# Expert outputs stored in two channel halves, their two planes summed by matrix products, and the loop for further tokens placed ahead of the last expert's down products

## The chip, the cores and the metric

The kernel runs on one core of one Trainium2 chip. The metric is device time in microseconds (us) of one launch. The core has five engines that run their own instruction streams in order and wait on semaphores: PE (TensorE, matrix products), DVE (VectorE), ACT (ScalarE), POOL (GpSimd) and SP (SyncE, which only issues transfers here). Sixteen DMA engines move data between memory and SBUF.

## The reference, cut to what matters

Two blocks of a network run on 512 tokens of 1,024 channels. The first ends in a mixture of 32 experts: each token goes to two of them, and the two results, each weighted, are added to the residual stream.

```python
def hierarchical_moe(h, ...):
    ...                                   # two experts and two gates for each token
    def run_block(args):                  # one expert on the tokens that chose it
        tok, e = args
        xb = hf[jnp.minimum(tok, n_tok - 1)]
        a = xb @ w_gate[e]
        b = xb @ w_up[e]
        return (jax.nn.silu(a) * b) @ w_down[e]
    out = lax.map(run_block, (slot_tok..., block_expert))
    out = out * slot_gate[:, None]
    y = zeros.at[slot_tok].add(out)       # each token: the sum of its two experts' rows

x = x + gate_f * hierarchical_moe(h, ...)
return rms_norm(x, final_g)               # end of the first block
# the second block begins:
x = x + gmlp_mixer(rms_norm_2(x, a_norm), a_w_in, ...)   # uv = gelu(h @ w_in): 1024 -> 2048
```

## The kernel before

**Layout.** Activations are kept with channels on the partitions (`xT`, eight tiles of 128 channels x 512 tokens). Most matrix products run as three (`mm3`): each operand is split into a rounded part and its remainder by ACT (the rounded part, `act`, line 416) and DVE (the remainder, `stt` or `tt`, lines 427 and 419). All code is written in the order in which each engine runs it (`manual_schedule`); nothing reorders it later.

**The experts** (`experts`) run as 19 units; a unit is one expert with up to 128 tokens or a pair with 64 each. Weights stream in through a ring of 15 places (`Ring`, lines 340 and 346, issued by SP). For a unit, the token rows are gathered from memory (line 1493, POOL), turned, multiplied by the gate and up weights, gated, turned again (`act_t`), and multiplied by the down weights (`down`) in two channel halves of 512 (`g` = 0, 1). DVE copies each half from PSUM into `yo` while multiplying by `gate_f`, and when both halves are there POOL scatters the rows with one indirect transfer (`scatter`, line 1498) into `y2` in memory: 2 x 512 rows of 1,024 channels, a plane for a token's first expert and a plane for its second. Ahead of the last unit's `act_t` and `down`, `self.ws.fill()` lets SP request the next stage's first two weight tiles (line 240, 1,024 KB each).

**The loop for further tokens** (`overflow`, line 1612) follows. It serves experts that got more tokens than a unit holds. Its count is read from memory by every engine (line 1611); in the profiled run it is zero, so that no instruction of its body runs. The loop's frame makes every engine wait, on entry and exit, for the semaphores of all transfers issued before it and for all engines.

**Combining** (`combine`) reads the two planes back for each of four tiles of 128 tokens, in twelve transfers on SP and ACT (line 1675); POOL adds the planes (line 1686, once DVE), PE turns each 128 x 128 piece (line 1689), DVE adds it to `xT`, and ACT and DVE make the split operand `ht`.

**The next stage** (`gmlp`) multiplies the 512 tokens by `a_w_in`. For `g` = 0 and 1 the group of products is 2 x 16 units: `ci` = 0, 1 (channels 0 to 511, then 512 to 1023), four channel tiles `i`, four token tiles `o`, three products each, 96 in a group. In the first group with `ci` = 0 the order is by token tile, and `ahead(o)` puts the combining of the following token tile in front of the products:

```python
if ci == 0 and ahead and i == 0:
    ahead(o)
```

Two norms need sums of squares over all channels (`stats_add`: a square by ACT, an addition by DVE, for each channel tile and each of two norms, 16 in all). They are queued in `self.late` when the last token tile has been combined, and taken one at each unit by `factors`, which after 21 units has PE sum them over the partitions (16 products of one column) and DVE compute `rcol`, the factor that the results of both groups need.

Of the kernel before, what the change touches and what calls it, by code (L numbers as in the profile page):

```python
# [10 lines left out]
F32 = mybir.dt.float32  # L11
# [3 lines left out]
OP = mybir.AluOpType  # L15
AX = mybir.AxisListType

S = 512
D = 1024
NT = 4  # L20
# [348 lines left out]
class Kern:  # L369
# [204 lines left out]
    def group(self, specs, acts, banks, weights_stationary=True, start=True, stop=True, done=None, ahead=None):  # L574
# [921 lines left out]

    def scatter(self, y, idx):
        self.nc.gpsimd.indirect_dma_start(out=self.y2[:, :], out_offset=bass.IndirectOffsetOnAxis(ap=idx, axis=0),
                                          in_=y, in_offset=None, bounds_check=2 * S - 1, oob_is_err=False)

# [11 lines left out]
    def experts(self):  # L1512

        nc = self.nc
        self.y2 = self.dr.tile([2 * S, D], F32, name="y2")
        self.ring.fill()
# [85 lines left out]
        self.ws.fill()  # L1602
        act_t(NU - 1)
        down(NU - 1)
        self.ws.hold = len(self.ws.order)
        self.ws.run()

    def overflow(self):
# [3 lines left out]
        with tc.For_i(0, n, 1) as i:  # L1612
# [47 lines left out]
            self.gated(yo, yb, ga)  # L1660
            self.scatter(yo, si[:, 0:1])

    def combine(self):

        nc = self.nc
        ya = [[self.slot(2 * t + k, [128, D]) for k in range(2)] for t in range(NT)]
        for t in range(NT):  # L1670
            n = 2 if t < 2 else 1
            for a in range(n):
                c = slice(a * D // n, (a + 1) * D // n)
                for k in range(2):
                    (nc.sync if k else nc.scalar).dma_start(ya[t][k][:, c], self.y2[k * S + t * 128:k * S + (t + 1) * 128, c])
# [4 lines left out]
        def tile(t):  # L1680
            c = slice(t * 128, (t + 1) * 128)
            b = Pair(*[self.bank(i) for i in ((6, 7), (0, 1))[t % 2]])
            xs = [self.xT[:, 4 * a:4 * a + 4, c] for a in range(2)]
            for a in range(2):
                y, y2 = (ya[t][k][:, a * 512:a * 512 + 512] for k in range(2))
                (nc.vector if (t, a) == (3, 1) else nc.gpsimd).tensor_tensor(out=y, in0=y, in1=y2, op=OP.add)  # L1686
            for a in range(2):
                for i in range(4):
                    nc.tensor.transpose(b[:, a, i * 128:i * 128 + 128], ya[t][0][:, a * 512 + i * 128:a * 512 + i * 128 + 128],  # L1689
                                        self.const("ident"))  # L1690
                self.tt(xs[a], b[:, a].rearrange("p (b t) -> p b t", b=4), xs[a], OP.add)
            for i in range(4):
                self.act(ht[i][:, :, 0, c], xs[i // 2][:, 2 * (i % 2):2 * (i % 2) + 2])
            for i in range(4):
                self.tt(ht[i][:, :, 1, c], xs[i // 2][:, 2 * (i % 2):2 * (i % 2) + 2], ht[i][:, :, 0, c], OP.subtract)

        return hl, tile
# [4 lines left out]
    def gmlp(self, hl, tile):  # L1702
# [6 lines left out]
        rcol = self.sb("rcol", [128, NT])  # L1709
        f = {}  # L1710
# [18 lines left out]

        def ahead(t):  # L1730

            if t == 0:
                tile(0)
            if t < NT - 1:
                tile(t + 1)
            if t == NT - 2:
                for dt in range(DT):
# [11 lines left out]
        for g in range(2):  # L1749
            bk = self.banks4(g)  # L1750

# [4 lines left out]

            self.group(self.HALVES, hl, bk, weights_stationary=False, done=done, ahead=None if g else ahead)
        self.drain()
# [351 lines left out]
def build(nc, ap, where):  # L2110
    with tile.TileContext(nc) as tc, ExitStack() as ctx:
# [4 lines left out]
        K.experts()  # L2116
        K.overflow()
        hl = K.gmlp(*K.combine())
# [22 lines left out]
```

## Time and profile before

| | |
|---|---|
| runs of the kernel | 1903.95, 1904.25, 1905.43 us; median 1904.25 us |
| the profiled execution | 1902.73 us, its span 1901.0 us |
| PE busy in the span | 1803.2 us, 95% |
| last down products of the experts begin / end | 740.95 / 744.60 us |
| first product of the next stage | 761.06 us |
| last of its first 192 products done, third group begins | 812.61 us |

Times within the execution count from the start of the span. The profile names an instruction by engine, source line, operation and its tiles (output <- inputs). "Idle before" is the time for which the engine had nothing to run, and the name behind it is what ended that. A queue's own instructions (waits, branches, requests for transfers) carry a q: SPq, PEldq.

### The profile page before, as it was taken

How to read it: one execution, taken by the hardware profiler on the slowest of the kernel's cores; microseconds unless marked ns; L12 is line 12 of the kernel's file. 1: busy time of each engine (PE TensorE's matmuls, PEld its weight loads, DVE VectorE, ACT ScalarE, POOL GpSimd, SP SyncE). 2: the span in 40 equal slices, each digit the busy share in tenths (PEclk: the TensorE clock that was granted, in tenths of full speed). 3: DMA queues.
4: the chain of work that ended last, by engine and by line, in shares of the span. 5: the costliest groups of instructions: out<-in, count | busy, mean ns of one | idle time of the engine just before them, and what ended most of it. 6: DMA issues, size and time to landing. Idle time of an engine off the chain costs nothing.

```text
span 1901.0 us, 21164 instructions
## 1 busy us (share of the span) xinstructions
PE 1803.2 (95%) x8110; PEld 1265.7 (67%) x8110; DVE 850.3 (45%) x1603; ACT 574.9 (30%) x1021; POOL 105.4 (6%) x101
## 2 busy tenths in 40 slices
PE   5988989999989995999999999999999999999997
PEld 4866654444333332788888888887778888888885
DVE  7668841111111111776545234355665654424434
ACT  4555320000000001633333123246666443222221
POOL 3430001000000001000000000000000000000000
PEclk9999889999999998999999999999999999999998
DMA  7534799999999997313222322322111222322221
GB/s 239 223 133 150 273 391 421 420 420 421 421 413 419 402 410 312 121 67 113 108 90 89 111 89 89 100 78 89 55 58 67 89 89 91 109 89 93 107 78 56
DMA packets 66280, 360.77 MB, mean 190 GB/s; under 512 B 10210, under 2 KB 10242, under 8 KB 33410
## 3 DMA queue, kind: packets, MB, share of 16 engines
q1 hardware_dynamic: 59184, 347.81, 47.6%
q0 software_dynamic: 5552, 8.44, 1.3%
q10 hardware_dynamic: 1442, 3.15, 0.4%
q8 instruction: 64, 1.05, 0.2%
q14 instruction: 38, 0.31, 0.0%
HBM read 356.42 MB, written 14.16 MB: 195 GB/s over the span
## 4 chain that ended last, share of the span: by engine, by line
PE 59%; DVE 1%; DMA 0%; ACT 0%; issue 0%; POOL 0%; ACTq 0%; DVEq 0%; POOLq 0%
PE q L407 58%; PE q L2018 0%; PE q L478 0%; DVE t L419 0%; DMA a<-y 0%; DVE a L427 0%; DVE xT L419 0%; DMA y<-a,sidx 0%; DVE w L427 0%; PE q L1689 0%; DVE ht L427 0%; DVE a L419 0%; ACT t L416 0%; POOL a L1686 0%; DVE sqacc L419 0%
## 5 line engine op out<-in xcount | busy, mean ns | idle before, releaser
L407 PE MATMUL q<-t,w 128*128 128x512 f32 (+1 forms) x3192 | 765.5, 397 | 5.8 <-ACT t L416 2.3
L407 PEld LDWEIGHTS q<-t,w 128*128 128x128 f32 (+1 forms) x3192 | 595.2, 189 | 147.1 <-issue 14.7
L419 DVE TENSOR_TENSOR w<-r,w 128x1024 fp32r<-128x1024 f32 (+1 forms) x173 | 208.7, 1226 | 306.8 <-ACT w L416 306.6
L407 PE MATMUL q<-a,w 128*128 128x512 f32 x1440 | 339.1, 395 | 0.0
L407 PEld LDWEIGHTS q<-a,w 128*128 128x128 f32 x1440 | 269.7, 188 | 63.6 <-issue 1.0
L416 ACT ACTIVATE w<-r 128x1024 fp32r<-128x1024 f32 (+1 forms) x173 | 177.2, 1049 | 348.0 <-issue 177.7
L407 PE MATMUL q<-r,a 128*64 128x512 f32 (+4 forms) x352 | 152.4, 569 | 4.2 <-DMA r<-in_we 4.2
L427 DVE SCALAR_TENSOR_TENSOR a<-a,gates,q 128x512 f32<-128x512 f32 x19 | 14.2, 747 | 277.3 <-PE q L407 264.0
L407 PE MATMUL q<-w,t 128*128 128x256 f32 (+1 forms) x672 | 122.1, 337 | 0.0
L416 ACT ACTIVATE gs<-q 128x512 f32<-128x512 f32 (+2 forms) x25 | 13.6, 544 | 351.4 <-PE q L1559 348.1
L407 PE MATMUL q<-t,a 128*64 128x512 f32 (+1 forms) x296 | 112.1, 596 | 7.0 <-DMA t<-in_we 5.3
L407 PEld LDWEIGHTS q<-w,t 128*128 128x128 f32 x672 | 102.9, 191 | 17.9 <-issue 4.1
L407 PE MATMUL q<-w,a 128*64 128x512 f32 x272 | 98.0, 596 | 11.4 <-DMA w<-in_we 11.4
L407 PE MATMUL q<-a,a 128*64 128x512 f32 (+7 forms) x424 | 98.3, 467 | 0.0
L407 PEld LDWEIGHTS q<-r,a 128*64 128x64 f32 (+1 forms) x352 | 52.7, 158 | 53.7 <-issue 44.0
L407 PEld LDWEIGHTS q<-t,a 128*64 128x64 f32 (+1 forms) x296 | 37.0, 152 | 64.9 <-issue 54.7
L419 DVE TENSOR_TENSOR a<-q,sqt 128x512 f32<-128x512 f32 x38 | 26.3, 691 | 115.1 <-PE q L407 110.2
L416 ACT ACTIVATE a<-ht 128x512 fp32r<-128x512 f32 (+1 forms) x60 | 37.8, 633 | 99.6 <-DVE ht L419 74.8
L419 DVE TENSOR_TENSOR xT<-q,xT 128x512 f32<-128x512 f32 x64 | 43.7, 686 | 53.4 <-PE q L407 43.5
L407 PEld LDWEIGHTS q<-a,a 128*128 128x128 f32 (+2 forms) x424 | 46.3, 173 | 30.6 <-issue 24.6
L407 PEld LDWEIGHTS q<-w,a 128*64 128x64 f32 x272 | 29.0, 137 | 55.1 <-issue 34.7
L427 DVE SCALAR_TENSOR_TENSOR w<-r,cols,w 128x256 fp32r<-128x256 f32 x96 | 44.4, 480 | 39.3 <-ACT w L416 39.1
(335 smaller groups left out, 1580.4 us busy)
## 6 DMA issues: line engine op xcount, KB each, us to landing
r<-in_w SPq DMA_DIRECT2D x100, 1024.0 KB, 4.9
t<-in_we SPq DMA_DIRECT2D x52, 1024.0 KB, 13.6
r<-in_we SPq DMA_DIRECT2D x52, 1024.0 KB, 17.9
w<-in_we SPq DMA_DIRECT2D x52, 1024.0 KB, 16.6
a<-in_we SPq DMA_DIRECT2D x72, 512.0 KB, 14.7
r<-in_w_ada SPq DMA_DIRECT2D x48, 512.0 KB, 5.0
r<-in_wa SPq DMA_DIRECT2D x8, 466.0 KB, 5.7
r<-in_w SPq DMA_DIRECT2D x5, 512.0 KB, 3.6
```

The costliest lines, as they stand in the source:

```text
L407: self.nc.tensor.matmul(out, lhsT=l, rhs=r, start=start, stop=stop)
L416: return self.nc.scalar.activation(out, in_, f, **kw)
L419: return self.nc.vector.tensor_tensor(out=out, in0=a, in1=b, op=op)
L427: return self.nc.vector.scalar_tensor_tensor(out, a, s, b, op0=op0, op1=op1, **kw)
```

## The change

1. `y2` becomes two arrays of 512 channels, `y2[0]` and `y2[1]`. `scatter` takes the half `g` and is called within the loop over `g`: two indirect transfers of half the row where there was one of the whole.
2. `overflow()` is called between `act_t(NU - 1)` and `down(NU - 1)`; the splitting of the next stage's first weights (`ws.hold`, `ws.run`) moves from the end of `experts` into `combine`, behind the requests for the first half.
3. `combine` reads a half-tile (128 tokens, both planes, 512 channels) in one transfer, eight in all: for half 0 on SP and ACT in turn, for half 1 on SP.
4. POOL's additions go. PE turns each piece by a product with the identity, and the second plane's product adds into the same PSUM place: eight products of 128 x 128 for a half-tile (line 407), where there were four transposes.
5. `ahead` now comes in both `ci` of the first group, with half-tiles: the products with channels 0 to 511 need only half 0. `factors` takes two of the statistics at each unit, eight when half 0 is combined and eight when half 1 is, then has PE sum them; the second group's third and fourth token tiles take the PSUM banks 0 and 1 once `r1` is there.

```diff
-            if ci == 0 and ahead:
+            if ahead:
                 units = [(i, o) for o in range(4) for i in range(len(kts))]
...
-                if ci == 0 and ahead and i == 0:
-                    ahead(o)
+                if ahead and i == 0:
+                    ahead(ci, o)
...
-    def scatter(self, y, idx):
+    def scatter(self, y, g, idx):
...
-        self.y2 = self.dr.tile([2 * S, D], F32, name="y2")
+        self.y2 = [self.dr.tile([2 * S, 512], F32, name=f"y2{g}") for g in range(2)]
...
-            self.scatter(yo, self.sidx[:, i:i + 1])
+                self.scatter(yo, g, self.sidx[:, i:i + 1])
...
         act_t(NU - 1)
+        self.overflow()
         down(NU - 1)
-        self.ws.hold = len(self.ws.order)
-        self.ws.run()
...
+        places = ((0, 1, 2, 4), (6, 7, *((5, 3) if NU % 2 else (3, 5))[::-1]))
+        ya = [[None] * NT for _ in range(2)]
+        for a in range(2):
+            src = self.y2[a][:, :].rearrange("(k t p) c -> t p k c", k=2, t=NT)
+            for t in range(NT):
+                ya[a][t] = self.slot(places[a][t], [128, 2, 512])
+                (nc.scalar if a == 0 and t % 2 else nc.sync).dma_start(ya[a][t], src[t])
+            if a == 0:
+                self.ws.hold = len(self.ws.order)
+                self.ws.run()
...
+            b = self.bank((0, 1, 6, 7)[t])
+            x = self.xT[:, 4 * a:4 * a + 4, c]
             for i in range(4):
-                self.act(ht[i][:, :, 0, c], xs[i // 2][:, 2 * (i % 2):2 * (i % 2) + 2])
...
+                for k in range(2):
+                    self.mm(b[:, i * 128:i * 128 + 128], ya[a][t][:, k, i * 128:i * 128 + 128], self.const("ident"), k == 0, k == 1)
+            self.tt(x, b.rearrange("p (b t) -> p b t", b=4), x, OP.add)
...
-            for _ in range(21):
-                yield
-                if self.late:
-                    self.late.pop(0)()
-            b = self.ps(2)
+            while f["stats"] < 2 * DT:
+                yield
+                for _ in range(2):
+                    if self.late:
+                        self.late.pop(0)()
+                        f["stats"] += 1
+            yield
+            b = Pair(self.bank(0), self.bank(1))
...
-        def ahead(t):
...
+        def ahead(a, t):
...
+            n = NT * a + t
+            if n == 0:
+                tile(0, 0)
+            if n < 2 * NT - 1:
+                tile((n + 1) // NT, (n + 1) % NT)
+            if n in (NT - 1, 2 * NT - 2):
+                for dt in range(4 * a, 4 * a + 4):
                     self.late.append(lambda d=dt: self.stats_add(xT[:, d], d))
...
+            if n == NT - 1:
                 self.bg.append(factors())
...
-        K.overflow()
```

**Place one: PE's stream around the loop.** `q_790`, `q_791` (changed: `q_812`, `q_813`) are the last unit's two down halves, `gs` its activations, `r_` and `t_` the down weights, `a_817` (`a_815`) the first rows read back. Before:

```order
L1559 MATMUL q_788_4202<-cst_70,a_782_4171 128x128 [waits DVE_49]
...
L407 MATMUL q_790_4209<-r_767_4090,gs_4207 64x512 [waits DMAHW4_49,DVE_49,Activation_49]
...
L407 MATMUL q_791_4210<-t_776_4122,gs_4207 64x512 [waits DMAHW6_49,DVE_49]
...
L1611 TENSOR_LOAD overi_3757 [waits DVE_49]
L1612 COMPARE_AND_BRANCH
...
L1612 REGISTER_ALU
...
L1689 MATMUL q_843_4411<-cst_70,a_817_4370 128x128 [waits Pool_49]
```

After the change; the row that ends the loop is where every engine leaves it (`DMAHW` are the semaphores of SP's and ACT's transfers, `DMASW` those of POOL's):

```order
L1560 MATMUL q_788_4257<-cst_70,a_782_4223 128x128 [waits DVE_49]
...
L1611 TENSOR_LOAD overi_3797 [waits DVE_49]
L1612 COMPARE_AND_BRANCH
...
L1612 REGISTER_ALU
L1612 COMPARE_AND_BRANCH
L1612 UNCONDITIONAL_BRANCH [waits DMASW5_49,DMASW4_49,DMASW6_49,DMASW3_49,DMASW7_49,DMASW2_49,DMAHW0_49,DMASW1_49,DMAHW1_49,DMASW0_49,DMAHW2_49,SP_sequencer_49,DMAHW3_49,DVE_sequencer_49,DMAHW4_49,PE_sequencer_49,DMAHW5_49,Activation_s
L407 MATMUL q_812_4394<-r_767_4139,gs_4262 64x512
...
L407 MATMUL q_813_4395<-t_776_4174,gs_4262 64x512
...
L407 MATMUL q_843_4468<-cst_70,a_815_4421 128x128 [waits DMAHW1_49]
```

The loop has moved ahead of the last unit's down products, and the combining now follows those products directly.

**Place two: SP's stream before the loop, the same in both kernels but for the numbers.** `r_786` and `r_787` are the next stage's first weight tiles. After the change:

```order
L340 DMA t_776_4174<-in_we 128x2048
L340 ISA
L340 DMA t_779_4190<-in_we 128x2048
L240 DMA r_786_4253<-in_w 128x2048
L240 DMA r_787_4255<-in_w 128x2048
L1611 TENSOR_LOAD overi_3797
...
L1612 REGISTER_ALU
...
L1676 DMA a_815_4421<-y_1976 128x2x512
L1676 DMA a_817_4425<-y_1976 128x2x512
L1676 DMA a_821_4439<-y_1977 128x2x512
```

Nothing moved ahead of the loop: the two weight tiles are requested before it, as before, and stand now between the loop's exit and the last down products.

**Place three: PE's stream at the statistics.** `q_862` is the turning of the last half-tile (half 1, tokens 384 to 511), `q_838` and `q_839` the third and fourth token tile of the first group, `q_871` and `q_872` the sums of squares. Changed kernel:

```order
L407 MATMUL q_862_4682<-cst_70,a_824_4445 128x128 x8
L407 MATMUL q_838_4462<-w_841_4466,t_827_4449 128x512
...
L407 MATMUL q_839_4463<-w_841_4466,t_827_4449 128x512
L407 MATMUL q_839_4463<-w_842_4467,t_827_4449 128x512
L407 MATMUL q_839_4463<-w_841_4466,t_827_4449 128x512
L407 MATMUL q_871_4735<-cst_70,sqacc_4590 128x1 x4
L407 MATMUL q_872_4736<-cst_70,gs_4592 128x1 x4
```

Between the turning of the last half-tile and the sums PE has five units, 15 products. Before the change the last turning stood 21 units ahead of the sums.

## Rows read from the trace of the kernel before

**Rows 1.** The page: busy time by engine; the chain that ended last.

```profile
PE 1803.2 (95%) x8110; PEld 1265.7 (67%) x8110; DVE 850.3 (45%) x1603; ACT 574.9 (30%) x1021; POOL 105.4 (6%) x101
...
PE 59%; DVE 1%; DMA 0%; ACT 0%; issue 0%; POOL 0%; ACTq 0%; DVEq 0%; POOLq 0%
```

**Rows 2.** Windows, us: busy per engine, PE's clock, DMA share, GB/s.

```profile
735.00:740.00 5.00, 4.48 (x18) 1.33 (x18) 0.69 (x1) 0.47 (x1) 0.98 (x1) 1.00 0.66 267
740.00:745.00 5.00, 3.67 (x15) 1.05 (x14) 0.36 (x1) 1.45 (x3) 0.00 (x0) 1.00 0.15 61
745.00:750.00 5.00, 0.00 (x0) 0.00 (x0) 2.98 (x5) 1.11 (x2) 1.23 (x1) 0.69 0.04 11
750.00:755.00 5.00, 0.13 (x1) 0.14 (x2) 0.00 (x0) 0.00 (x0) 1.26 (x1) 0.50 0.92 305
760.00:765.00 5.00, 4.71 (x15) 3.94 (x16) 5.00 (x8) 2.56 (x6) 4.02 (x4) 0.60 1.04 419
```

**Rows 3.** Timeline: start, duration, instruction, idle before and who ended it.

```profile
729.26 0.34 SPq L240 DMA_DIRECT2D r<-in_w  x1
...
734.12 0.66 PE L1559 MATMUL q<-cst,a 128*128 128x128 f32 x4
...
740.95 3.65 PE L407 MATMUL q<-t,gs 128*64 128x512 f32 x14 [0.93 <-SPq L1612]
...
744.64 0.69 DVE L419 TENSOR_TENSOR a<-q,sqt 128x512 f32<-128x512 f32 x1 [4.73 <-PE q L407]
...
745.61 1.23 POOL L1498 DMA_INDIRECT y<-a,sidx  x1 [9.43 <-DVE a L419]
749.12 5.33 SPq L1675 DMA_DIRECT2D a<-y  x6
...
753.55 1.26 POOL L1686 TENSOR_TENSOR a<-a,a 128x512 f32<-128x512 f32 x1 [6.71 <-DMA a<-y]
...
755.62 2.52 POOL L1686 TENSOR_TENSOR a<-a,a 128x512 f32<-128x512 f32 x2 [0.81 <-DMA a<-y]
...
761.06 4.35 PE L407 MATMUL q<-w,t 128*128 128x512 f32 x12
...
765.25 1.03 PE L1689 MATMUL q<-cst,a 128*128 128x128 f32 x8
...
772.08 0.63 PE L1689 MATMUL q<-cst,a 128*128 128x128 f32 x4 [2.57 <-DVE a L1686]
```

**Rows 4.** Line 1612, the loop's frame: durations ns min/median/max, first and last start.

```profile
L1612 SPq EVENT_SEMAPHORE  x19: 17/28/5623, 730.4 to 748.9; - x19
...
L1612 PEldq COMPARE_BRANCH  x3: 92/174/192, 741.7 to 749.3; - x3
```

**Rows 5.** Line 240, window 729 to 730.5: the second weight tile.

```profile
DMA to landing us min/median/max: 16.8/16.8/16.8
```

**Rows 6.** Line 1498, window 745 to 746: the last scatter.

```profile
DMA to landing us min/median/max: 2.8/2.8/2.8
```

**Rows 7.** Line 1498, window 735 to 736: the scatter before it.

```profile
DMA to landing us min/median/max: 7.6/7.6/7.6
```

**Rows 8.** Timeline of PE, later: products in a stream, and 128 x 128 products.

```profile
792.66 20.11 PE L407 MATMUL q<-w,t 128*128 128x512 f32 x88
812.61 4.92 PE L407 MATMUL q<-t,w 128*128 128x512 f32 x21
...
841.31 1.50 PE L407 MATMUL q<-a,a 128*128 128x128 f32 x12
```

**Rows 9.** Timeline at the statistics: DVE's and ACT's steps, first square, last addition, PE's sums.

```profile
769.92 1.41 DVE L427 SCALAR_TENSOR_TENSOR w<-r,fa,w 128x512 fp32r<-128x512 f32 x2
...
772.57 0.72 ACT L416 ACTIVATE t<-xT 128x256 fp32r<-128x256 f32 x2 [2.07 <-DVE xT L419]
772.75 0.69 DVE L419 TENSOR_TENSOR xT<-q,xT 128x512 f32<-128x512 f32 x1 [0.21 <-PE q L1689]
...
774.10 0.62 ACT L416 ACTIVATE sqacc<-xT 128x512 f32<-128x512 f32 x1
...
786.95 0.68 DVE L419 TENSOR_TENSOR gs<-gs,sqt 128x512 f32<-128x512 f32 x1
...
787.55 0.95 PE L407 MATMUL q<-cst,sqacc 128*128 128x1 f32 x8
...
789.25 0.93 PE L407 MATMUL q<-w,t 128*128 128x512 f32 x3
```

**Rows 10.** DMA queues, window 746.5 to 749: the last scatter alone.

```profile
q0 software_dynamic: 144, 0.04, 6.1%
```

More of the change, by code (lines that the diff above doesn't have):

```diff
@@ L1495, in gather @@
                                           bounds_check=S - 1, oob_is_err=False)
-    def scatter(self, y, idx):
-        self.nc.gpsimd.indirect_dma_start(out=self.y2[:, :], out_offset=bass.IndirectOffsetOnAxis(ap=idx, axis=0),
-                                          in_=y, in_offset=None, bounds_check=2 * S - 1, oob_is_err=False)
+    def scatter(self, y, g, idx):
+        self.nc.gpsimd.indirect_dma_start(out=self.y2[g][:, :], out_offset=bass.IndirectOffsetOnAxis(ap=idx, axis=0),
+                                          in_=y[:, g * 512:(g + 1) * 512], in_offset=None, bounds_check=2 * S - 1, oob_is_err=False)
     def turned(self, x, b):
@@ L1660, in overflow @@
             self.gated(yo, yb, ga)
-            self.scatter(yo, si[:, 0:1])
+            for g in range(2):
+                self.scatter(yo, g, si[:, 0:1])
     def combine(self):
         nc = self.nc
[L1669 to L1675, printed above, removed]
+        places = ((0, 1, 2, 4), (6, 7, *((5, 3) if NU % 2 else (3, 5))[::-1]))
[8 more added lines that the diff above has]
+                self.ws.run()
         self.ws.stop = len(self.ws.order)
@@ L1678, in combine, with tile @@
         hl = [(ht[d // 2][:, d % 2, 0], ht[d // 2][:, d % 2, 1]) for d in range(DT)]
-        def tile(t):
+        def tile(a, t):
             c = slice(t * 128, (t + 1) * 128)
[L1682 to L1691, printed above, removed]
-            for i in range(4):
-                self.act(ht[i][:, :, 0, c], xs[i // 2][:, 2 * (i % 2):2 * (i % 2) + 2])
-            for i in range(4):
-                self.tt(ht[i][:, :, 1, c], xs[i // 2][:, 2 * (i % 2):2 * (i % 2) + 2], ht[i][:, :, 0, c], OP.subtract)
+            b = self.bank((0, 1, 6, 7)[t])
+            x = self.xT[:, 4 * a:4 * a + 4, c]
+            for i in range(4):
+                for k in range(2):
+                    self.mm(b[:, i * 128:i * 128 + 128], ya[a][t][:, k, i * 128:i * 128 + 128], self.const("ident"), k == 0, k == 1)
+            self.tt(x, b.rearrange("p (b t) -> p b t", b=4), x, OP.add)
+            for i in range(2):
+                self.act(ht[2 * a + i][:, :, 0, c], x[:, 2 * i:2 * i + 2])
+            for i in range(2):
+                self.tt(ht[2 * a + i][:, :, 1, c], x[:, 2 * i:2 * i + 2], ht[2 * a + i][:, :, 0, c], OP.subtract)
         return hl, tile
@@ L1709, in gmlp @@
         rcol = self.sb("rcol", [128, NT])
-        f = {}
+        f = {"stats": 0}
         def factors():
-            for _ in range(21):
+            while f["stats"] < 2 * DT:
                 yield
-                if self.late:
-                    self.late.pop(0)()
-            b = self.ps(2)
+                for _ in range(2):
[4 more added lines that the diff above has]
+            b = Pair(self.bank(0), self.bank(1))
             r1 = self.sb("rf1", [128, NT])
@@ L1728, in factors @@
             f["r1"] = r1
-        def ahead(t):
[L1732 to L1737, printed above, removed]
+        def ahead(a, t):
[6 more added lines that the diff above has]
+                for dt in range(4 * a, 4 * a + 4):
                     self.late.append(lambda d=dt: self.stats_add(xT[:, d], d))
                     self.late.append(lambda d=dt: self.stats_add(xT[:, d], d, "gs", scale=self.col("final_g", d)))
+            if n == NT - 1:
                 self.bg.append(factors())
@@ L1749, in gmlp, with others @@
         for g in range(2):
-            bk = self.banks4(g)
+            if g == 0:
+                bk = self.banks4(0)
+            else:
+                self.half = 0
+                p = self.ps(2)
+                bk = [p[:, 0], p[:, 1], None, None]
+            def others(ci, t, bk=bk):
+                if (ci, t) == (0, 2):
+                    while "r1" not in f:
+                        self.step()
+                    bk[2:] = self.bank(0), self.bank(1)
             def done(t, bk=bk, g=g):
@@ L1755, in done @@
                 self.act(v[t][:, g * 512:(g + 1) * 512], bk[t], AF.Gelu_apprx_tanh, scale=rcol[:, t:t + 1])
-            self.group(self.HALVES, hl, bk, weights_stationary=False, done=done, ahead=None if g else ahead)
+            self.group(self.HALVES, hl, bk, weights_stationary=False, done=done, ahead=others if g else ahead)
         self.drain()
```

## Prediction

> **What bounds the kernel now.** I read the page first. PE is busy for 1803.2 us, 95% of the span, and the chain that ended last has 59% of the span on PE and at most 1% on any other engine [rows 1]. So a change pays by PE time taken out or by PE's idle time taken away, and it costs PE time put in and new idle time.
>
> The windows around the junction of the experts and the next stage then show where PE stands idle here: it has 0.00 us of 5 in 745 to 750 and 0.13 in 750 to 755, and its granted clock falls from 1.00 to 0.69 and to 0.50, the lower level, and is 0.60 in 760 to 765 [rows 2]. The timeline gives the links: the last down products end at 744.60 us, DVE multiplies (0.69), POOL issues the scatter (1.23 from 745.61), SP's first read of the planes comes at 749.12, the rows land at 753.55 and 755.62, POOL adds (1.26 each), PE turns, and the first product of the next stage starts at 761.06 [rows 3]. From there to the start of the third group at 812.61 [rows 8] PE has a nearly unbroken stream, and behind 812.61 nothing that the change touches stands. So I work out when the first product would start, and what lies between it and the third group. All that follows is added to the profiled execution's own 1902.73 us; the median of the runs is 1.5 us above it.
>
> **Term 1: the loop now waits ahead of the down products.** Its frame costs little by itself when everything has landed (the last branch takes 0.17 us), but SP's waits in it last until 748.9, with one of 5.6 us [rows 4]. It waits for every transfer issued before it. In its new place the last of these are the next stage's two weight tiles, which are requested ahead of it at 729.26 [rows 3]; the second lands 16.8 us later, at 746.1 [rows 5]. How long the loop takes to let go I read from its old place: the last scatter lands 2.8 us after 745.61, at 748.4 [rows 6], and PE's last branch starts at 749.3 [rows 4], about 1.0 us later. So PE would start the down products at about 747.1. In the kernel before they could start at 735.5, behind the turning at 734.12 (0.66 us) [rows 3] and an ACT copy. Nothing covers this wait: PE's, DVE's and ACT's next work all stands behind the same loop.
>
> **Term 2: the down products.** The last half took 3.65 us at full clock [rows 3], and the halves are equal. PE would have stood still for 12 us before them, and after such a stop the clock was 0.50 [rows 2], so half 0 takes between 3.65 and twice that. When PE began anew at 761.06, the window's mean of 0.60 means that the clock was at 0.50 until about 764.0, some 2.9 us [rows 2, 3]. With 2.9 us at half speed, 1.5 us are lost: half 0 is done at 747.1 + 3.65 + 1.5 = 752.3 (bounds 750.75 and 754.4). Half 1 runs behind it, under the wait for half 0's rows.
>
> **Term 3: the rows and back.** From the end of the products to the landing of the scatter took 744.60 to 748.4, 3.8 us [rows 3, 6]; I take 3.9, since no loop stands behind it now, only a semaphore. The reads come to 4.4 us for the first (749.12 to 753.55) and 6.5 for the one behind it (to 755.62) [rows 3]. PE's first product needs two half-tiles turned, 512 KB each on two queues, about what those landings brought; I take 6.4 us for the later one. A turning of eight products (0.9 us), DVE's addition and the operand's split come to 1.3 before the first product can run. So the next stage starts at 752.3 + 3.9 + 6.4 + 1.3 = 763.9, where it was 761.06: **+2.8 us**. With half 0's bounds, 4.4 for the reads and 0.9 to 1.7 for the turning it is +0.3 to +5.5. The removed POOL additions are in this: their 1.26 us each are gone, and the loop's wait takes more than that back.
>
> **Term 4: from the first product to the third group.** Before, these 51.55 us hold 192 products at 0.2267 us (88 of them start to start, 792.66 to 812.61 [rows 8]), 43.5; 16 transposes at 0.109 (eight in 1.03, less 0.16 for the last one's depth), 1.75; PE's sums, 787.55 to 789.25 [rows 9], 1.7; one wait of 2.57 for POOL's and DVE's additions [rows 3]; about 1.45 lost to the low clock; and 0.55 of rest.
>
> After, there are the same 43.5, 1.7 and 0.55. Six half-tiles are turned and summed here, with eight products of 128 x 128 each. The trace has such products on plain 4-byte operands, 12 in 1.50 us, so 0.112 each with the same depth off [rows 8]: 48 x 0.112 = 5.4. The low clock takes 1.0 (0 to 1.9), since the turnings and half 1 have run before. The new part is a wait. Two statistics at a time, eight squares and eight additions stand between the last half-tile's addition and PE's sums, and PE has only 15 products there, 3.4 us, and the turning itself, 0.9: 4.3 us. In the other engines' chain stand the turning (0.9) with its way to DVE (0.25, an estimate), DVE's addition (0.69) and the rounded part on ACT (0.72), and then eight squares and additions. A square takes 0.62 and an addition 0.68 [rows 9]; at 0.69 for each they need 5.5 us, and at the pace of before (774.10 to 787.63 for 16, 0.85 each [rows 9]) 6.8. That is 8.1 to 9.4 us, less the 4.3 that PE has: a wait of 3.8 to 5.1. I take 5.0, near the pace of before, since DVE has splits of the next weights in between (1.41 for two [rows 9]). Before the change the sums stood 21 units behind the last turning, and the last addition (to 787.63) met the sums (from 787.55) without a wait. A further 1.0 (0 to 2) goes to DVE's backlog: it was busy for all 5.00 us of 760 to 765 [rows 2], and has an addition (0.69), two splits of operands and its share of the statistics and of the weights' splits for each half-tile, while PE has 3.6 us of work. Sum: 43.5 + 5.4 + 1.7 + 0.55 + 1.0 + 6.0 = 58.15, **+6.6 us**, with 0 to 1.9 for the clock and 3.8 to 8 for the waits +3.4 to +9.5.
>
> **Term 5: twice as many scatters.** Nineteen more indirect transfers run while the weights stream. The last scatter, alone, took 6.1% of 16 engines for 2.5 us, or 0.15 us of them all [rows 10]; the one before it, among weights, needed 7.6 us to land [rows 7], which nothing waits for there. If half a row costs no less than a whole one, the stream of weights ends 19 x 0.15 = 2.9 us later; if the bytes decide, nothing changes. I take **+0.4**, near the end of the bytes: the bytes are the same, and where the DMA share was 0.66 [rows 2] there is room for some of the rest. The Trainium skill ("DMA: Bandwidth & Descriptors", Rules for kernel authors) says that small transfers should be coalesced, since under 64 KB one pays mostly overhead; by it the halves would cost as much as whole ones, and the sum would be 2.5 us higher. No row here shows a scatter of half a row.
>
> **The sum.** 2.8 + 6.6 + 0.4 = 9.8 us: the profiled execution would come to 1912.5, and the median, 1.5 above, to **1914**. I round up to 1914.2 as the bounds lie wider above than below. The case's own range is 1909 to 1919.
>
> **The rivals.** *The loop lets go early* (chance 0.10, the other side). If the weight tiles land earlier in their new company, or the loop doesn't wait for them, PE goes on at 735.5, half 0 ends at 739.2, its rows are in memory at 743.0 (747.8 if the scatter takes 7.6, among the weights [rows 7]), and the first product starts at 750.7 (755.5). That is 10.4 (5.6) us early, less the 7.0 of terms 4 and 5: 1900.8 (1905.7). For it speaks that half 1 hides behind half 0's way; against it that SP's requests stand ahead of the loop and the loop waits for all of its queue's semaphores. The point that decides: the first product follows the release by 15.25 us (3.65 + 3.9 + 6.4 + 1.3), and must come before 754.1 to repay 7.0, so the release must come before 738.8. The weights' landing at 746.1 [rows 5] says no.
>
> *No wait for the statistics* (0.10): squares and additions slip into ACT's and DVE's idle time as fast as they come, and PE's 15 products suffice. Then 5.0 us go, and the time is 1909.2.
>
> *Summing by products costs more* (0.05): if an exact 4-byte product passed four times where the rounded one passes once, 128 columns would take 4 x 0.2267 / 4 = 0.227 instead of 0.112, and 48 of them 5.5 us more, 1919.7. The 12 products of [rows 8] speak against it. The Trainium skill ("FP8 and Floating Point Precision", TensorE Precision Notes) has this rule, four passes for true FP32; the trace's 0.112 is half of what it gives, and a transpose costs the same 0.109 here.
>
> **How the numbers follow.** The forecast has 0.75. About 0.2%, 3.8 us, is what a measurement of this kernel tells from no change, so "same" ends at 1908.1. The early loop gives 0.06 faster and 0.04 same; no wait for the statistics reaches into the same with 0.04; the forecast's lower end adds 0.02; and 0.02 more goes to faster for what I have not seen. Faster 0.08, same 0.10, slower 0.82. The range reaches down to between the statistics' rival and the early loop, 1907, and up to the dearer products, 1920.
>
> **What would show it.** Right: PE idle from 734.8 to about 747 in front of the last down products, with a loop's instruction named as what ended it; a granted clock near 0.5 to 0.7 in 747 to 755; the first product of the next stage near 764; a PE wait of about 5 us for DVE or ACT in front of the products of one column; the third group's start near 822; no POOL additions. Wrong: down products at 736, or sums without a wait. What would spoil it most is the weight tiles' landing time, since terms 1 to 3 hang on it one to one.

## The result and the profile after

The changed kernel takes 1920.93 us (median of four runs, 1917.11 to 1922.68) where the kernel before takes 1904.1 (four runs, 1902.4 to 1905.43). The ratio is 1.0085, with a 95% interval of 1.0073 to 1.0097: slower by 14 to 18 us. The direction was forecast; the time lies 6.7 us above the forecast of 1914.2 and 0.9 us above the upper end of the range.

The profiled execution took 1922.68 us, the slowest of the four, its span 1920.9. From the third group on nothing has changed (from its start to the end of the span 1088.4 us before, 1087.8 after), so the loss lies ahead of it. The timeline of PE, with one row of SP, in the changed kernel (start, duration, instruction, idle before and what ended it):

```profile
730.43 0.34 SPq L240 DMA_DIRECT2D r<-in_w  x1
...
735.30 0.66 PE L1560 MATMUL q<-cst,a 128*128 128x128 f32 x4
748.33 6.40 PE L407 MATMUL q<-r,gs 128*64 128x512 f32 x16 [12.38 <-issue]
754.57 3.60 PE L407 MATMUL q<-t,gs 128*64 128x512 f32 x16
762.61 6.18 PE L407 MATMUL q<-cst,a 128*128 128x128 f32 x32 [4.44 <-DMA a<-y]
768.55 2.98 PE L407 MATMUL q<-w,t 128*128 128x512 f32 x12
771.37 1.95 PE L407 MATMUL q<-cst,a 128*128 128x128 f32 x16
773.07 2.99 PE L407 MATMUL q<-w,t 128*128 128x512 f32 x12
...
794.08 1.95 PE L407 MATMUL q<-cst,a 128*128 128x128 f32 x16
795.78 3.68 PE L407 MATMUL q<-w,t 128*128 128x512 f32 x15
803.27 1.83 PE L407 MATMUL q<-cst,sqacc 128*128 128x1 f32 x8 [3.81 <-DVE sqacc L419]
804.97 1.84 PE L407 MATMUL q<-cst,gs 128*128 128x1 f32 x8
806.67 26.56 PE L407 MATMUL q<-w,t 128*128 128x512 f32 x105
833.07 4.92 PE L407 MATMUL q<-t,w 128*128 128x512 f32 x21
```

In the kernel before the first half of the last down products followed the turning after 0.75 us:

```profile
735.52 3.65 PE L407 MATMUL q<-r,gs 128*64 128x512 f32 x16 [0.75 <-ACT gs L416]
```

Against this line and [rows 3, 8, 9] the reader is to see four things. PE stands idle for 12.38 us ahead of the last down products. The trace does not name the loop as what ended that: `issue` means that no releaser shows. The first half of these products takes 6.40 us, the second, equal one 3.60. A half-tile's turning stands in 16 records, not eight, and lasts 1.70 us from its start to the products behind it (771.37 to 773.07). And PE waits 3.81 us for the statistics' additions, after which the sums take 1.70 us for each eight records (803.27 to 804.97) where all 16 took 1.7 before. (The order has four and four products for these sums, so the "16 products of one column" above are 16 records of eight products.)

The waits of SP's queue from 730 to 750 (us in all, times, longest) name the only transfers in its waits there, the next stage's weight tiles (10.5 us more are put down to the queue itself, so x2 below has to decide):

```profile
SPq L1612 <- DMA r<-in_w: 4.2, 2, 2.4
```

The windows (columns as in [rows 2]; the third number from the end is PE's granted clock, 0.50 its lower level) show the clock behind each of the three idle times:

```profile
745.00:750.00 5.00, 1.67 (x4) 0.53 (x6) 0.00 (x0) 0.00 (x0) 0.00 (x0) 0.50 0.05 18
750.00:755.00 5.00, 5.00 (x17) 1.47 (x14) 0.21 (x1) 0.00 (x0) 0.00 (x0) 0.61 0.00 0
755.00:760.00 5.00, 3.17 (x16) 0.84 (x12) 1.41 (x3) 1.00 (x2) 1.79 (x2) 1.00 0.18 35
760.00:765.00 5.00, 2.39 (x11) 2.39 (x12) 2.50 (x4) 1.56 (x3) 0.17 (x1) 0.57 1.03 388
765.00:770.00 5.00, 5.00 (x29) 4.76 (x29) 2.14 (x4) 1.17 (x4) 0.00 (x0) 0.74 0.65 234
...
800.00:805.00 5.00, 1.73 (x9) 1.76 (x9) 3.69 (x6) 2.98 (x5) 0.00 (x0) 0.67 0.10 41
805.00:810.00 5.00, 5.00 (x17) 4.32 (x18) 3.97 (x25) 0.00 (x0) 0.59 (x1) 0.50 0.00 0
```

Three times PE stops and goes on at the clock's lower level: at 748, at 762 and at 803. The second was there before [rows 2]; the first and the third are new.

One thing has to be set apart in all that follows. The start of the last expert's turning (T, line 1559 or 1560) lay between 732.65 and 737.15 us in the 14 profiles of this study, though the code ahead of it hardly differs. I therefore compare two stretches of a profile: from T to the first product of the next stage (M), and from M to the third group's start (G). They are differences of starts in each timeline. Before: 26.94 and 51.55, 78.49 together. After: 33.25 and 64.52, 97.77. The change costs 6.3 us ahead of M and 13.0 behind it. Each stretch is read from one profile of each kernel, so it carries no interval.

### The profile page after: what moved, and what is told of

Same layout as the page of the kernel before. It is cut to its first block, busy times and chain, and to the rows that moved or that the text cites. A ratio compares the mean times of both kernels' runs of the same rounds, so it can differ in the third digit from the quotient of the medians.

```text
span 1920.9 us, 21387 instructions
## 1 busy us (share of the span) xinstructions
PE 1820.3 (95%) x8206; PEld 1280.6 (67%) x8206; DVE 848.3 (44%) x1602; ACT 575.6 (30%) x1021; POOL 114.9 (6%) x113
## 4 chain that ended last, share of the span: by engine, by line
PE 74%; DMA 16%; DVE 6%; ACT 2%; issue 1%; SPq 0%; DVEq 0%; POOLq 0%; ACTq 0%
PE q L407 72%; DMA a<-in_we 4%; DMA r<-in_we 4%; DMA t<-in_we 4%; DMA w<-in_we 3%; DMA r<-in_w 1%; ACT a L416 1%; DVE r L427 1%; DVE w L419 1%; DVE ht L427 1%; DMA xT<-in_x 0%; PE q L2034 0%; PE q L478 0%; PE q L1539 0%; ACT sqt L416 0%
## 5 line engine op out<-in xcount | busy, mean ns | idle before, releaser
L407 PEld LDWEIGHTS q<-w,t 128*128 128x128 f32 x672 | 103.5, 192 | 17.9 <-issue 4.1
L407 PE MATMUL q<-r,gs 128*64 128x512 f32 (+1 forms) x128 | 53.5, 643 | 14.5 <-issue 12.4
L1499 POOL DMA_INDIRECT y<-a,sidx x38 | 39.4, 1037 | 421.8 <-DVE a L419 404.2
```

The lines of the kernel that those rows point to most:

```text
L407: self.nc.tensor.matmul(out, lhsT=l, rhs=r, start=start, stop=stop)
L1499: self.nc.gpsimd.indirect_dma_start(out=self.y2[g][:, :], out_offset=bass.IndirectOffsetOnAxis(ap=idx, axis=0), in_=y[:, g * 512:(g + 1) * ...
```

## The experiments

Times are medians; the ratio is that of each kernel to the kernel before on the same chip, with its 95% interval. The kernel before had medians of 1904.1 to 1904.94 us beside these runs, so a difference between two rows' times is good to about 1 us.

| run | time, us | ratio | T to M | M to G | T to G |
|---|---|---|---|---|---|
| before | 1904.1 | 1 | 26.94 | 51.55 | 78.49 |
| the change | 1920.93 | 1.0085 (1.0073 to 1.0097) | 33.25 | 64.52 | 97.77 |
| x1 loop back | 1914.26 | 1.0047 (1.0033 to 1.0061) | 25.30 | 64.73 | 90.03 |
| x2 weight tiles behind the loop | 1916.75 | 1.0062 (1.0048 to 1.0075) | 26.97 | 64.56 | 91.53 |
| x3 sums later | 1912.18 | 1.0038 (1.0026 to 1.005) | 33.50 | 56.44 | 89.94 |
| x4 POOL adds | 1920.17 | 1.0078 (1.0064 to 1.0091) | 31.10 | 63.81 | 94.91 |
| x5 before, halves only | 1905.56 | 1.0001 (0.9992 to 1.001) | 25.73 | 54.67 | 80.40 |
| x6 products in the wait at the sums | 1918.14 | 1.0072 (1.0058 to 1.0085) | 33.23 | 60.40 | 93.63 |
| x8 loop back, sums later, POOL adds | 1906.35 | 1.0006 (0.9997 to 1.0015) | 22.90 | 58.38 | 81.28 |
| x10 loop back, sums later | 1904.84 | 1.0007 (0.9998 to 1.0016) | 24.92 | 56.41 | 81.33 |
| x11 as x10, 10 products behind the loop | 1904.15 | 0.9999 (0.999 to 1.0008) | 22.91 | 56.41 | 79.32 |
| x12 as x8, statistics one at a unit | 1903.94 | 0.9995 (0.9986 to 1.0004) | 22.93 | 57.25 | 80.18 |
| x13 as x12, 18 products behind the loop | 1905.6 | 1.0004 (0.9995 to 1.0013) | 24.06 | 56.20 | 80.26 |
| x14 before, 18 products behind the loop | 1904.93 | 1.0 (0.9991 to 1.001) | 27.84 | 53.38 | 81.22 |

My theory was that the loss has three places: the loop's wait for the weight tiles with the low clock behind it, PE's turnings by 4-byte products, and the wait at the sums. The rivals were that the loop's place costs nothing by itself, that twice as many scatters are the cause, and that ACT and DVE, not PE, set the pace.

**x1, the loop back.**

```diff
         act_t(NU - 1)
-        self.overflow()
         down(NU - 1)
+        self.overflow()
```

> The change, with the loop for further tokens back behind the last down products (the only edit). Theory (the loop's place costs by the second weight tile's landing and by the low clock behind it): the down products start near 736.7 instead of 748.3 and run at full clock, the rows come back behind the loop at about 754 and the first product of the next stage starts near 761 instead of 768.6; 7 to 8 us less, about 1913. Rival (the loop's place is worth nothing, since the halves' way through memory takes as long behind the loop): within 1 us of the changed kernel, 1920 to 1922.

The time fell by 6.7 us and T to M by 7.95. PE's timeline:

```profile
734.05 3.97 PE L407 MATMUL q<-r,gs 128*64 128x512 f32 x16 [0.75 <-ACT gs L416]
...
739.65 3.65 PE L407 MATMUL q<-t,gs 128*64 128x512 f32 x14 [1.09 <-SPq L1612]
751.58 6.62 PE L407 MATMUL q<-cst,a 128*128 128x128 f32 x32 [8.28 <-DMA a<-y]
757.95 2.98 PE L407 MATMUL q<-w,t 128*128 128x512 f32 x12
```

The down products run at once and at full clock. The rest of the change is left in, and M to G stays at 64.7. PE still waits 8.28 us for the rows, and the turnings behind that wait run at the low clock (6.62 us). So the loop's place costs 7 to 8 us, and it costs them ahead of M alone.

**x2, the weight tiles requested behind the loop.**

```diff
-        self.ws.fill()
         act_t(NU - 1)
         self.overflow()
+        self.ws.fill()
         down(NU - 1)
```

> The change, with the next stage's two weight tiles requested behind the loop instead of ahead of it (the only edit). Theory (those tiles are what the loop waits for): the loop ends near 743, with the last scatter's landing, and the last down products start some 4 us earlier, near 744; the first product of the next stage 4 to 5 us earlier and the time about 1916. Rival (the loop has a cost of its own or waits for the scatters as long): the down products start within 1 us of 748.3 and the time stays.

The waits of SP's queue, 730 to 750, and PE's next products:

```profile
SPq L1612 <- DMA y<-a,sidx: 5.2, 2, 4.0
```

```profile
743.99 5.62 PE L407 MATMUL q<-r,gs 128*64 128x512 f32 x16 [7.72 <-issue]
```

The tiles no longer end the wait; the scatters among the last weights (`y<-a,sidx`) do, and PE's idle time is 4.7 us shorter. The time fell by 4.2 us, T to M by 6.3. That the tiles held the loop is shown, and also that without them it would still hold PE for 7.7 us.

**x3, the sums later.**

```diff
-            yield
+            for _ in range(7):
+                yield
             b = Pair(self.bank(0), self.bank(1))
```

> The change, with PE's sums of squares six units (18 products, 4.1 us) later (the only edit). Theory (PE waits 3.8 us for the statistics and then has half its clock for the sums and the products behind them): no wait, the clock stays at 1.00, the sums take 1.7 instead of 3.4 us; 3.8 + 1.7 + about 2 less, 7 to 8 us, about 1913. Rival 1 (only the wait counts): 3.8 us less, 1917. Rival 2 (ACT and DVE are the bound and the wait only moves): less than 1 us.

```profile
794.46 7.76 PE L407 MATMUL q<-w,t 128*128 128x512 f32 x33
802.07 0.95 PE L407 MATMUL q<-cst,sqacc 128*128 128x1 f32 x8
802.87 1.03 PE L407 MATMUL q<-cst,gs 128*128 128x1 f32 x8
803.77 20.01 PE L407 MATMUL q<-w,t 128*128 128x512 f32 x87
```

PE's timeline has no wait, the sums take 1.7 us, and M to G fell by 8.1; the time fell by 8.75. The wait's own 3.81 us are less than half of its price.

**x6, products in the place of that wait** tells the other part apart. It adds 16 rounded products of 128 x 512 whose result is not read:

```diff
+            q = self.bank(6)
+            for k in range(16):
+                self.mm(q, hl[0][0][:, 0:128], hl[0][0], k == 0, k == 15)
             b = Pair(self.bank(0), self.bank(1))
```

> The change, with 16 products of 128 x 512 (3.6 us) whose result nobody reads ahead of PE's sums, in the place of the wait of 3.8 us. Theory (the wait's second half is the clock, which falls in it): the sums start at the same time, the clock stays at 1.00, they take 1.7 us instead of 3.4 and the products behind them run at full clock: 3.5 to 4.5 us less, about 1917. Rival (the clock is not lost by this wait): the low stretch stays, and the time is the same or up to 1 us longer.

```profile
798.87 3.79 PE L407 MATMUL q<-t 128*128 128x512 f32 x16
802.76 1.05 PE L407 MATMUL q<-cst,sqacc 128*128 128x1 f32 x8
803.67 1.03 PE L407 MATMUL q<-cst,gs 128*128 128x1 f32 x8
804.56 24.09 PE L407 MATMUL q<-w,t 128*128 128x512 f32 x105
```

The sums start as late behind the last turning as without them (9.1 us against 9.2), but PE worked up to them, they take 1.8 us instead of 3.4, and the products behind them 23.9 start to start instead of 26.4. M to G fell by 4.1, the time by 2.8. So of the 8 us that the sums cost, half is the wait and half the clock that it takes with it.

**x4, POOL's additions.**

```diff
-            for i in range(4):
-                for k in range(2):
-                    self.mm(b[...], ya[a][t][:, k, ...], self.const("ident"), k == 0, k == 1)
+            y = ya[a][t]
+            nc.gpsimd.tensor_tensor(out=y[:, 0], in0=y[:, 0], in1=y[:, 1], op=OP.add)
+            for i in range(4):
+                nc.tensor.transpose(b[...], y[:, 0, ...], self.const("ident"))
```

> The change, with the planes added by POOL and turned by four transposes for a half-tile (the only edit; the halves, the loop's place and the statistics stay). Theory (a 4-byte product of 128 x 128 is two records of 0.106 us each, so that a half-tile takes PE 1.70 instead of 0.44 us): the six half-tiles behind the first product take 7.6 us less, the first two 2 to 4 us less at the low clock against 1.3 to 2.5 for POOL; 8 to 10 us less, about 1912. Rival (ACT and DVE set the pace of the statistics, so that PE waits longer before the sums): the wait grows from 3.8 to 7 us or more and 3 to 6 us are saved, 1915 to 1918.

```profile
764.02 2.34 PE L1691 MATMUL q<-cst,a 128*128 128x128 f32 x8 [5.77 <-POOL a L1689]
766.37 5.29 PE L407 MATMUL q<-w,t 128*128 128x512 f32 x12
771.50 0.60 PE L1691 MATMUL q<-cst,a 128*128 128x128 f32 x4
771.85 3.00 PE L407 MATMUL q<-w,t 128*128 128x512 f32 x12
...
786.92 3.04 PE L407 MATMUL q<-w,t 128*128 128x512 f32 x12 [0.99 <-ACT t L416]
...
791.47 3.03 PE L407 MATMUL q<-w,t 128*128 128x512 f32 x12 [1.08 <-ACT t L416]
794.89 0.97 PE L407 MATMUL q<-w,t 128*128 128x512 f32 x3 [0.39 <-ACT t L416]
800.72 1.83 PE L407 MATMUL q<-cst,sqacc 128*128 128x1 f32 x8 [4.86 <-DVE sqacc L419]
```

A half-tile's turning now takes 0.35 us (771.50 to 771.85) instead of 1.70, and little is gained: 0.8 us of the time, within the spread of its runs, and in the profile 2.2 of T to M and 0.7 of M to G. The six turnings behind M are 8.1 us shorter together. Against that, PE waits for ACT at four half-tiles (3.2 us with one of 0.72 earlier) and 4.86 us instead of 3.81 at the sums, and behind a wait of 5.77 for POOL's additions the first twelve products run at the low clock (5.1 us start to start where the change has 2.8). My theory that undoing the dear turnings pays by itself falls. The rival has the right engines, but not its numbers: it had a wait of 7 us at the sums and 3 to 6 us saved, and it said nothing of the clock.

**x8 and x10** ask the same with the other two costs gone; x10 is x1 and x3 together, x8 has x4's edit too.

> The change with two edits: the loop back behind the down products and the sums six units later, the summing by products kept. Theory (the two costs add): 6.7 + 8.7 us less than the changed kernel as measured one by one, about 1906, 1 to 3 us over the kernel before, and no wait at the sums. Rival (they overlap): 1908 or more.

> The change with three edits: the loop back behind the down products, the sums six units later, POOL's additions and four transposes for a half-tile. Theory (with the wait at the sums gone, PE's shorter turnings count): from the first product to the third group 64.7 becomes 50 to 53 us, and the time is 1899 to 1902, 2 to 5 us faster than the kernel before. Rival (ACT's and DVE's work for each half-tile, not PE's, sets the pace of this stage): PE waits for ACT at the half-tiles as it did with POOL's additions alone, and the time is that of the twin kernel that keeps the summing by products, 1905 to 1908.

The two costs add: x10 is 16.1 us under the change (x1 and x3 alone 6.7 and 8.75), and with 81.33 from T to G only 2.8 over the kernel before. x8, with POOL's additions, has 81.28. One of its half-tiles, turned at 775.25 and multiplied from 780.04, shows where a part of the shorter turnings' gain goes:

```profile
775.25 0.60 PE L1691 MATMUL q<-cst,a 128*128 128x128 f32 x4
...
777.54 0.69 DVE L419 TENSOR_TENSOR sqacc<-sqacc,sqt 128x512 f32<-128x512 f32 x1
778.25 0.69 DVE L419 TENSOR_TENSOR gs<-gs,sqt 128x512 f32<-128x512 f32 x1
...
778.86 0.68 DVE L419 TENSOR_TENSOR xT<-q,xT 128x512 f32<-128x512 f32 x1
779.57 0.72 ACT L416 ACTIVATE t<-xT 128x256 fp32r<-128x256 f32 x2 [1.36 <-DVE xT L419]
...
780.04 3.03 PE L407 MATMUL q<-w,t 128*128 128x512 f32 x12 [0.98 <-ACT t L416]
```

DVE adds the half-tile only at 778.86, behind the statistics' additions and without a gap; ACT waits for DVE, and PE for ACT. From M to G the turnings are 7.7 us shorter than in x10. Waits for ACT and DVE behind the first twelve products take back 4.9 us of it (start to start), the first twelve products 3.2 (5.99 against 2.82, at the low clock behind POOL's additions), and the 87 products behind the sums 1.6 (21.43 against 19.87; the granted clock of 790 to 800 is 0.83, in x10 1.00). So the pace of ACT and DVE is one half of the reason, and the clock is the other.

**x5, the halves alone,** in the kernel before: two arrays, two scatters of 512 channels for a unit, 16 reads.

```diff
-        self.y2 = self.dr.tile([2 * S, D], F32, name="y2")
+        self.y2 = [self.dr.tile([2 * S, 512], F32, name=f"y2{g}") for g in range(2)]
...
-            self.scatter(yo, self.sidx[:, i:i + 1])
+                self.scatter(yo, g, self.sidx[:, i:i + 1])
...
```

> The kernel before, with the expert outputs scattered in two halves into two arrays and read back from them in 16 transfers (the only edit; loop, POOL additions, order of the next stage as before). Theory (19 more scatters cost the weight stream nothing; the experts' end differs by up to 1.5 us from run to run anyway): within 1.5 us of the kernel before. Rival (a scatter of half a row costs the DMA engines as much as one of a whole row): the last turning of the experts 2 to 3 us later than in the runs before, and 2 to 4 us slower.

The ratio is 1.0001, and its interval ends 1.9 us above the kernel before, just under the 2 to 4 us of the rival, which falls. T lies at 736.16, inside the spread of the others. Twice as many scatters cost nothing that can be measured; a cost under 1.9 us is not excluded (T is 734.98 in the mean of the twelve profiles with half scatters, 734.12 and 732.90 in the two without, too few to tell).

**x11 to x14** look for a version that beats both, in what the three stretches at the low clock leave: unread products of 128 x 128 (4-byte) behind the loop, 10 in x11 and 18 in x13 and x14, keep PE at work until the rows come, and x12 takes the statistics one at a unit, with the sums four units behind the last. The edit of x11 against x10:

```diff
         self.overflow()
+        q = self.bank(1)
+        for k in range(10):
+            self.mm(q[:, 0:128], self.const("ident"), self.const("ident"), k == 0, k == 9)
```

> The loop back and the sums six units later, with 10 products of 128 x 128 (result unread) between the loop and the first turning, where PE stood idle 3.7 us. Theory (the 32 products of the first two turnings ran 6.0 us instead of 3.4 because the clock had fallen in the idle time): the first turning starts at the same time, the clock is back earlier and 2 to 3 us go, about 1902 to 1903. Rival (the clock does not come back in so short a stretch): no change.

```profile
750.89 4.13 PE L407 MATMUL q<-cst 128*128 128x128 f32 x20 [4.80 <-issue]
754.85 3.74 PE L407 MATMUL q<-cst,a 128*128 128x128 f32 x32
758.35 3.01 PE L407 MATMUL q<-w,t 128*128 128x512 f32 x12
```

In x11 the 32 records of the first two turnings take 3.5 us start to start instead of 5.8 in x10, and T to M falls by 2.0. The time is 1904.15, the same as before: T to G is 79.32 against 78.49.

The edit of x12 against the change, beside the loop's place and POOL's additions as in x8:

```diff
-                for _ in range(2):
-                    if self.late:
+                if self.late:
...
-            yield
+            for _ in range(4):
+                yield
```

> The loop back, POOL's additions with four transposes, and the statistics one at each unit instead of two, with the sums four units behind the last. Theory (ACT's and DVE's statistics in the middle of the half-tiles made PE wait for ACT, some 3 us in all): the waits before the half-tiles' products shrink and PE's 8.5 us less of turning show: 2 to 4 us under the twin with two at each unit, 1902 to 1904. Rival (the half-tiles' own addition, rounding and split are the bound): the waits stay and so does the time, 1906.

```profile
782.66 3.03 PE L407 MATMUL q<-w,t 128*128 128x512 f32 x12 [1.55 <-ACT t L416]
786.70 5.75 PE L407 MATMUL q<-w,t 128*128 128x512 f32 x24 [1.01 <-ACT t L416]
```

M to G fell by 1.1 and the wait at the sums is gone, but PE's waits for ACT are as long as before, at other half-tiles. The time, 1903.94, can't be told from x8's or from the kernel before.

> The kernel of the run before it, with 18 products of 128 x 128 (result unread) between the loop and the first turning, in 5.3 us of PE's idle time. Theory (the low clock costs there 1.3 us in the first turnings and about 2 in the first twelve products): 3 to 3.5 us less than without them, 1899 to 1901, faster than the kernel before. Rival: they delay the first turning or leave the clock as it is, no gain.

> The kernel before, with the same 18 unread products between the loop and the combining, where PE stood idle for 5.4 us behind the loop. Theory: the turnings and the first twelve products of the next stage run at full clock, 2 to 2.5 us less than before, 1901.5 to 1902. Rival (PE there waits for POOL and the transfers, not for its own clock): less than 0.7 us.

Both rivals are right. In x13 the 18 products take 6.8 us start to start (752.59 to 759.38) instead of the 5.3 that I had allowed, push the first turning back, and T to M grows by 1.1. They do bring the clock back: the first twelve products take 3.9 us start to start instead of x12's 5.95. But M to G falls by only 1.05, since PE's waits for ACT behind them grow from 2.9 to 4.1 us. That speaks for the pace of ACT and DVE once more. In x14 the clock comes back and is lost again, because PE then waits for POOL's additions:

```profile
759.97 1.11 PE L1689 MATMUL q<-cst,a 128*128 128x128 f32 x4 [2.40 <-POOL a L1686]
760.74 5.19 PE L407 MATMUL q<-w,t 128*128 128x512 f32 x12
```

None of the twelve beats the kernel before by more than the measurement tells.

## Why the prediction was wrong, point by point

The points are read from the profiled execution, which took 1922.68 us where the sum had put it at 1912.5, 10.2 us less. From T to M it grew by 6.3 us, above the bound of +5.5, and from M to G by 13.0, above +9.5. (The upper bounds, with 2.9 for the scatters, add up to 17.9 us or 1922, above the 1920 that I gave.) Two steps failed, each by about 7 us: the price of a plain 4-byte product, and the clock behind PE's waits. Two terms that came out smaller hid a part of it.

**Term 1, the loop's wait: right.** I had the down products at 747.1; they began at 748.33, and T and the tiles' request were 1.2 us later in this profile, so that the term is right to 0.1. x2 shows that the weight tiles held the loop, as I had argued. The early loop, the rival on the other side, did not happen. The sign that I had named, a loop's instruction as what ended PE's wait, is not in the trace, which has `issue` there; x2 stands in for it.

**Term 2, the down products at the low clock: right in kind, too small.** I let the low clock last 2.9 us and half 0 take 5.15; the windows have 0.50 in 745 to 750 and 0.61 in 750 to 755, and half 0 took 6.4. That is 1.25 us. The 2.9 us were misread. They count from 761.06, but PE had begun anew at 754.87, with its turnings:

```profile
754.87 1.11 PE L1689 MATMUL q<-cst,a 128*128 128x128 f32 x4 [10.27 <-POOL a L1686]
```

So 2.9 us are the end of a low stretch and not its length after a new start; here the windows' means put its end at about 753.9, 5.6 us behind PE's start at 748.33.

**Term 3, the rows' way and the first turnings: two errors against each other.** From half 0's end to PE's first turning I had 3.9 + 6.4 = 10.3 us; the rows have 7.9 (748.33 + 6.40 = 754.73 to 762.61). The turnings, for which I had 1.3 us with what follows them, took 5.94 (762.61 to 768.55). I had counted eight products there; PE ran 16 ahead of M, each at twice the price that I used. That would be 3.4 us at full clock; the other 2.5 are the low clock (0.57 in 760 to 765, 0.74 in 765 to 770). M came at 768.55, not at 763.9. The term's lower bound was also added up wrongly: 750.75 + 3.9 + 4.4 + 0.9 is 759.95, 1.1 us before the kernel before and not 0.3 behind it.

**Term 4, the price of a turning: this is the first step that failed.** "12 in 1.50 us, so 0.112 each" [rows 8] takes a row's count for a count of products. Plain 4-byte products stand in the trace as two records each: the order has eight for a half-tile and the trace 16, and x11's ten added products have the row `x20`, while x6's 16 rounded ones have `x16`. The very group of [rows 8] says so too. In the source line 1808 makes 8 x 4 = 32 of these products, and the trace of the kernel before has 64 records of them (PE by form, 824 to 860):

```profile
L407 PE MATMUL q<-a,a 128*128 128x128 f32 x64 | 9.4, 274 | 0.0
```

So the 12 records in 1.50 us were six products. One costs 1.70 / 8 = 0.213 us, and 48 of them 10.2 us of PE, where I had 5.4. I gave 0.05 to the rival that says so, with a time of 1919.7, and held these very 12 records against it. The Trainium skill ("FP8 and Floating Point Precision", TensorE Precision Notes) has four passes for true FP32. The trace agrees, with 0.213 against 0.2267 / 4 = 0.057 for 128 columns of a rounded product, 3.75 times as much.

**Term 4, the statistics: the wait was right, and the clock behind it, the second step that failed, was put at nothing.** I had a wait of 5.0 and a DVE backlog of 1.0; the trace has 3.81 in one wait. What I left out is the clock, though the same prediction lets it fall in the wait ahead of the down products: the sums took 3.4 us instead of 1.7, and 105 products 26.4 instead of 23.8. x3 gives 8.1 us back for the whole and x6 4.1 for the clock alone.

The parts of M to G against mine: turnings +4.8, wait and backlog -2.2, sums +1.7, clock +1.6 (2.6 where I had 1.0); together 5.9 of the 6.4 us between 58.15 and 64.52.

By kind, and with the stretch ahead of M: the number and price of the plain products came to 6.9 us more than I had (2.1 ahead of M, 4.8 behind it). The low clock cost 9.6 us (2.75 in half 0, 2.5 in the first turnings, 1.7 in the sums, 2.6 behind them) where I had 2.5, 7.1 more. The rows' way gave 2.4 back and the wait 2.2. With the right number and price of these products and all else as it was, the forecast would have been 1919 to 1921, near the measured time, but in part by luck, since the clock's error and the terms that came out smaller would still be in it.

**Term 5, the scatters:** 0.4 forecast, nothing measurable in x5, whose interval holds 0.4 and excludes 2.9. The scatter that I priced was a light one: it moved 0.04 MB [rows 10], while the 18 gathers and 18 scatters from 260 to 745 us moved 8.16 MB, 0.23 MB each.

A right price of the turnings would not have said what they are worth when undone. Shorter turnings save 7.7 to 8.1 us of PE time, but with POOL's additions PE's waits for ACT and DVE and its low clock take back as much (x4, and x8 against x10), so undoing them brings nothing. x1 and x3, which undo the loop's place and the place of the sums, bring 16.1 us together of the 16.8 (x10). What stays open is how much ACT's or DVE's order could still give in x8: x12 moved PE's waits and did not remove them.

## What to carry to other kernels

A frame that waits for all transfers is to stand where nothing big is in flight; request the next stage's tiles behind it, or leave the frame where its wait lies under another one. An idle stretch of PE is to be priced with what it does to the clock: here a wait of 3.8 us cost 8. Before a price is read from a grouped row, hold the row's count against the order of the program, and before PE time is bought or sold, look which engine feeds that PE work.

## What was not expected of the hardware

- A plain 4-byte product is two records of 0.106 us at 128 columns, a transpose of the same tile one of 0.109.
- Unread products brought the clock back for good where PE had work right behind them: T to M fell by 2.0 us in x11. In x14 the first twelve products took 5.19 us after a new wait of 2.40, longer than the 4.35 of [rows 3].
- The end of the experts' stage differs by up to 4.5 us between profiles (T from 732.65 to 737.15), although PE's work ahead of it is the same; the times of one kernel spread by more (1900.78 to 1907.1 in x5).
